# Start addresses in SBUF of the operands of the weight products, in a hybrid attention, SSD and short-convolution kernel

## The chip, the cores and the metric

The kernel runs on one core of one Trainium2 chip. The metric is the time of one execution in device microseconds. Before the change it is 1823.35 us, the median of three runs (1823.07 to 1825.55). All inputs and the output are float32.

## The reference, cut to what matters

Two layers over 256 latent tokens of width 2048, with 256 context tokens beside the first:

```
h  = modulate(rms_norm(x, g0), shift, scale)          # shift, scale, gate = split(silu(c) @ ada_w + ada_b)
hc = modulate(rms_norm(ctx, g0), shift_c, scale_c)
p  = h @ w_in ;  pc = hc @ w_in[:, COL_K:]            # w_in: 2048 x 14400
ya = neighbourhood_attention(q, k, v, k_ctx, v_ctx) * silu(gate_a)     # 16 heads of 128
yb = gated_group_rmsnorm(bidirectional_ssd(...) + d * xs, z)           # 32 heads of 64, state 128
x  = x + gate * (concat(ya, yb) @ w_out)              # w_out: 4096 x 2048
h1 = modulate(rms_norm(x, g1), shift1, scale1)
bg, cg, hv, g = split(h1 @ sc_in, 4)                  # sc_in: 2048 x 8192
x  = x + gate1 * ((silu(g) * bg * dw_conv(cg * hv)) @ sc_out)          # sc_out: 2048 x 2048
```

Nearly all of the arithmetic is in the products with `w_in`, `w_out`, `sc_in` and `sc_out`.

## The kernel before

**Products in two parts.** A float32 product is made of three products of TensorE's faster float32r type. A weight tile (1024 columns in 128 partitions, 512 KB) is loaded into a `raw` buffer, rounded to float32r by ScalarE (`split`, L399, into one of three tiles `wH`), and the rest is found by VectorE (`low_part`, L406, into one of three tiles `wL`). Activations are split in the same way into `hH[kb]` and `hL[kb]`, for the 16 blocks `kb` of 128 input channels ("k-blocks"). Then high x high, high x low and low x high are summed in a PSUM bank:

```
mm(o, actH[:, tt], H, first, False)          # mm_act: activations stationary, 512 weight columns move
mm(o, actH[:, tt], Lo, False, False)
mm(o, actL[:, tt], H, False, last)
mm(o, H[:, bb], actH[:, :n], f, False)       # mm_ws: weights stationary, n = 256 or 512 tokens move
mm(o, H[:, bb], actL[:, :n], False, False)
mm(o, Lo[:, bb], actH[:, :n], False, last)
```

`mm` is the helper at L188 that records every product, and `turn` at L192 records every transpose. `proj` walks the 16 k-blocks in order and runs one of three forms: "act" (`mm_act`: Q, K and V of the attention, the output projection, `sc_out`), a width (`mm_ws`: 512 for B, C and X of the SSD, 256 for the gates), or "both" (`mm_both`: `sc_in`, where one product of 512 columns takes the high and the low half of an `h1` tile together against `wH`, and one of 256 takes the high half against `wL`). In "act" with four token tiles a k-block holds 4 x 3 products; in the 512 and 256 forms it holds 4 column blocks x 3.

**What sets the order.** The order on every engine is written out by a planner when the program is built: `Plan` keeps a clock for each engine and marks by tile and 128-element unit; side work (norms, attention heads, SSD chunks, the gemv of `ada_w` on VectorE) stands in generators that `pump` lets in between the products when their inputs are due. `issue` sends weight loads on SP's queue as soon as a `raw` buffer is free. ScalarE's queue issues a few DMAs; GpSimd issues none. The planner sees names of tiles and offsets inside them, never an address.

**Where tiles lie.** `st(shape, tag, ...)` asks the pool `sb` for a tile with one buffer. The pool gives a tag its place when the tag is first asked for, one after another in each of the 128 partitions, and later tiles with the same tag share the place. At the bottom lie 16384 bytes that the builder keeps for descriptors of DMAs that software would generate, and four small constants. So places follow from the order of the `st` calls: first `tmp`, `half`, `raw`, `wH`, `wL` and the attention buffers; then constants; `x_load` takes `hH0` to `hH7` for the rows of x; a small tile `bs1` and `Bl`, `Cl` follow, then `hL2` to `hL15` (as `xm`, the transposed x); later, when the context rows are loaded, `hH8` to `hH15`; and at last `hL0` and `hL1`. The tags are used again and again: `xs`, `hH`, `mix0` to `mix15` and `y2` share the places of `hH`; `xm`, `hL`, `mix16` to `mix31` and `h1` those of `hL`.

## Time and profile before

| | |
|---|---|
| median of the runs | 1823.35 us (1823.07 to 1825.55) |
| span of the profiled execution | 1819.0 us; the runs' median is 4.35 us above it, for what lies around the first and the last instruction |
| instructions | 26337 |
| loads of weights into `raw`, 512 KB each | w_in 209, ada_w 163, sc_in 128, w_out 64, sc_out 32 |
| moved by DMA | 376.90 MB, 207 GB/s over the span |
| splitting a weight tile | ScalarE 1044 ns, VectorE 1213 ns (440 of each) |

How to read it: a row of the profile's groups gives line, engine, operation, output<-inputs by the program's names without their numbers, shape, count, busy time, mean time of one in ns, and the idle time of the engine just ahead of them. PE is TensorE's products; PEld is its loading of stationary operands, which runs beside them. Products are pipelined, so that one "takes" 390 ns while the next starts 227 ns after it; the pace is read from starts, or from the busy time of a stretch without gaps, divided by the products that start in it. Stretches are given in us from the span's start.

### The profile page before, as it was taken

What the parts mean: (1) busy time and instruction counts of PE and PEld (TensorE: products, weight loads), DVE (VectorE), ACT (ScalarE), POOL (GpSimd) and SP (SyncE); (2) the same over time, 40 slices, a digit from 0 to 9 for tenths busy, and PEclk for the clock granted to TensorE, in tenths of its full rate; (3) what the DMA queues carried; (4) which work ended last, traced back from release to release, by engine and by line L of the source; (5) the groups of instructions that cost most, each with busy time, mean ns of one, the idle gap of its engine ahead of it and who ended that gap; (6) DMA issues with size and microseconds to landing.
All of it is one profiled execution on the core that took longest, in us unless ns stands there. A gap on an engine that the chain in (4) does not pass through costs nothing.

```text
span 1819.0 us, 26337 instructions
## 1 busy us (share of the span) xinstructions
PE 1779.8 (98%) x9961; PEld 1484.2 (82%) x9961; DVE 1259.4 (69%) x2041; ACT 775.3 (43%) x1362; POOL 30.5 (2%) x28
## 2 busy tenths in 40 slices
PE   5999999999999999999999999999999999999998
PEld 3677888878888878888877898787878888888887
DVE  5566775887575887575887687766768866565665
ACT  5322543455232455232454344543435444444442
POOL 0000100000000000000001000000000000000000
PEclk9999999999999999999999999999999999999999
DMA  9987654566655576755575566768876776666564
GB/s 321 344 290 251 202 167 130 165 211 206 206 164 172 163 222 198 218 163 173 166 221 181 166 183 179 219 217 287 272 248 199 237 232 189 189 193 188 193 209 152
DMA packets 249216, 376.90 MB, mean 207 GB/s; under 512 B 32656, under 2 KB 104048, under 8 KB 249088
## 3 DMA queue, kind: packets, MB, share of 16 engines
q1 hardware_dynamic: 239792, 366.64, 64.2%
q10 hardware_dynamic: 9296, 8.57, 1.4%
q8 instruction: 78, 1.28, 0.3%
q14 instruction: 50, 0.41, 0.1%
HBM read 368.70 MB, written 7.77 MB: 207 GB/s over the span
## 4 chain that ended last, share of the span: by engine, by line
PE 90%; DMA 5%; DVE 3%; issue 1%; ACT 1%; SPq 0%; ACTq 0%; POOLq 0%; POOL 0%; DVEq 0%
PE bank L188 87%; DMA raw<-in_ada_w 4%; PE bank L192 3%; DVE wL L406 1%; DMA tmp<-dram_mixd 1%; DVE acc L793 1%; DMA raw<-in_w_out 1%; ACT wH L399 0%; SPq L556 0%; DVE hL L742 0%; DVE tmp L738 0%; ACT mix L1486 0%; ACT hH L736 0%; DVE xm L602 0%; DVE tmp L1780 0%
## 5 line engine op out<-in xcount | busy, mean ns | idle before, releaser
L399 ACT CAST wH<-raw 128x1024 fp32r<-128x1024 f32 (+1 forms) x440 | 459.0, 1044 | 704.3 <-PE bank L188 550.8
L406 DVE TENSOR_TENSOR wL<-raw,wH 128x1024 fp32r<-128x1024 f32 (+1 forms) x440 | 531.9, 1213 | 264.1 <-ACT wH L399 261.7
L188 PE MATMUL bank<-h,wH 128*128 128x512 f32 x1024 | 358.0, 396 | 2.7 <-ACT h L1626 1.5
L188 PE MATMUL bank<-hH,wH 128*128 128x256 f32 (+1 forms) x1040 | 353.4, 340 | 0.9 <-ACT wH L399 0.9
L188 PE MATMUL bank<-hL,wH 128*128 128x256 f32 (+1 forms) x1040 | 338.1, 325 | 0.0
L188 PE MATMUL bank<-hH,wL 128*128 128x256 f32 (+1 forms) x1024 | 330.9, 323 | 0.8 <-DVE wL L406 0.8
L188 PE MATMUL bank<-h,wL 128*128 128x256 f32 x1024 | 285.0, 278 | 0.0
L188 PE MATMUL bank<-wH,hH 128*128 128x512 f32 x640 | 258.4, 404 | 4.7 <-ACT hH L736 2.6
L188 PE MATMUL bank<-wL,hH 128*128 128x512 f32 x640 | 250.8, 392 | 0.3 <-DVE wL L406 0.3
L188 PE MATMUL bank<-wH,hL 128*128 128x512 f32 x640 | 249.8, 391 | 0.1
L793 DVE SCALAR_TENSOR_TENSOR acc<-raw,csil,acc 128x512 f32<-128x512 f32 x256 | 191.9, 749 | 64.2 <-DMA raw<-in_ada_w 50.6
L188 PEld LDWEIGHTS bank<-h,wH 128*128 128x128 f32 x1024 | 192.1, 188 | 49.4 <-issue 2.2
L188 PEld LDWEIGHTS bank<-hH,wH 128*128 128x128 f32 x1040 | 196.5, 189 | 24.5 <-issue 7.5
L188 PEld LDWEIGHTS bank<-hL,wH 128*128 128x128 f32 x1040 | 196.9, 189 | 20.2 <-issue 5.3
L188 PEld LDWEIGHTS bank<-hH,wL 128*128 128x128 f32 x1024 | 194.0, 189 | 18.2 <-DVE wL L406 1.4
L188 PEld LDWEIGHTS bank<-h,wL 128*128 128x128 f32 x1024 | 192.7, 188 | 0.0
L188 PE MATMUL bank<-wH,mix 128*128 128x512 f32 x512 | 163.1, 394 | 1.0 <-ACT wH L399 1.0
L188 PEld LDWEIGHTS bank<-wH,hH 128*128 128x128 f32 x640 | 120.2, 188 | 36.3 <-issue 7.5
L188 PEld LDWEIGHTS bank<-wH,hL 128*128 128x128 f32 x640 | 120.2, 188 | 26.2 <-DVE hL L742 0.6
L188 PEld LDWEIGHTS bank<-wL,hH 128*128 128x128 f32 x640 | 120.2, 188 | 24.7 <-DVE wL L406 1.1
L188 PEld LDWEIGHTS bank<-wH,mix 128*128 128x128 f32 x512 | 96.2, 188 | 22.1 <-ACT wH L399 1.4
L188 PE MATMUL bank<-wL,mix 128*128 128x512 f32 x256 | 100.5, 392 | 5.2 <-DVE wL L406 5.2
(244 smaller groups left out, 1661.4 us busy)
## 6 DMA issues: line engine op xcount, KB each, us to landing
raw<-in_w_in SPq DMA_DIRECT2D x209, 512.0 KB, 4.5
raw<-in_ada_w SPq DMA_DIRECT2D x163, 512.0 KB, 4.8
raw<-in_sc_in SPq DMA_DIRECT2D x128, 512.0 KB, 3.7
raw<-in_w_out SPq DMA_DIRECT2D x64, 512.0 KB, 4.3
raw<-in_sc_out SPq DMA_DIRECT2D x32, 512.0 KB, 4.5
tmp<-dram_csr SPq DMA_DIRECT2D x32, 256.0 KB, 7.3
PT<-in_ada_w SPq DMA_DIRECT2D x14, 512.0 KB, 8.4
yi<-in_ada_w SPq DMA_DIRECT2D x8, 512.0 KB
```

Source lines behind the costliest of these rows:

```text
L188: E(T.matmul(o, l, r, start=start, stop=stop, skip_group_check=True))
L192: E(T.transpose(o, i, ident if k == 128 else ident[:k, :k]))
L399: E(S.copy(H, v))
L406: E(V.tensor_tensor(out=Lo, in0=v, in1=H.bitcast(F32), op=ALU.subtract))
L793: E(V.scalar_tensor_tensor(out=acc, in0=v[:, j], scalar=csil[:, 2 * k + j:2 * k + j + 1], in1=acc, op0=ALU.mult, op1=ALU.add))
```

## The change

Right after `st` is defined, all tiles that weight products read are asked for first, so that the pool lays them out from the bottom, and a pad ahead of them brings the first to byte 2048. The scratch for software DMAs shrinks from 16384 to 1024 bytes, which makes the start of the pool 1152 and gives the room for the pad.

```
+    sb.tile([128, 224], F32, tag="pad", name="pad", bufs=1)
+    for k in range(16):
+        st([128, 512], f"hH{k}", F32R)
+    for k in range(16):
+        st([128, 512], f"hL{k}", F32R)
+    for k in range(3):
+        st([128, 1024], f"wH{k}", F32R)
+    for k in range(3):
+        st([128, 1024], f"wL{k}", F32R)
...
-    nc = bacc.Bacc("TRN2", target_bir_lowering=False, num_devices=1)
+    nc = bacc.Bacc("TRN2", target_bir_lowering=False, num_devices=1, dynamic_dma_scratch_size=1024)
```

The start addresses in a partition (bytes), as the two programs have them:

| tiles | before | modulo 2048 | after | modulo 2048 |
|---|---|---|---|---|
| `hH0` to `hH7` | 145984 and on | 576 | 2048 and on | 0 |
| `hH8` to `hH15` | 204416 and on | 1664 | 18432 and on | 0 |
| `hL0`, `hL1` | 220800, 222848 | 1664 | 34816, 36864 | 0 |
| `hL2` to `hL15` | 166528 and on | 640 | 38912 and on | 0 |
| `wH0` to `wL2` | 66688 and on | 1152 | 67584 and on | 0 |
| `tmp`, and `half` in steps of 1024 | 16512 and on | 128 | 92160 and on | 0 |
| `raw`, `KT`, `QT`, `Vt`, `PT`, `xtm`, `yi`, `sz`, `gt` | 46208 and on | 1152 | 121856 and on | 1024 |
| `Bl`, `Cl` | 162432, 164480 | 640 | 197120, 199168 | 512 |

576 is 64 more than a multiple of 128; all other rows of before are 128 more than a multiple of 512 (the odd `half` tiles, 1152, too). A weight tile's slices start 2048 bytes apart (two blocks of 512 columns), its column blocks 512 bytes apart.

No instruction is added, removed or moved: with tile numbers and line numbers left out, the rows of all five engines and of their DMA queues, with their waits, are the same in both programs.

## The prediction

> **What bounds the kernel now.** The page is read first: the span, the busy shares, the granted clock, the queues and the chain of work that ended last.

> ```profile
> span 1819.0 us, 26337 instructions
> ...
> PE 1779.8 (98%) x9961; PEld 1484.2 (82%) x9961; DVE 1259.4 (69%) x2041; ACT 775.3 (43%) x1362; POOL 30.5 (2%) x28
> ...
> PEclk9999999999999999999999999999999999999999
> ...
> q1 hardware_dynamic: 239792, 366.64, 64.2%
> q10 hardware_dynamic: 9296, 8.57, 1.4%
> q8 instruction: 78, 1.28, 0.3%
> q14 instruction: 50, 0.41, 0.1%
> ...
> PE 90%; DMA 5%; DVE 3%; issue 1%; ACT 1%; SPq 0%; ACTq 0%; POOLq 0%; POOL 0%; DVEq 0%
> PE bank L188 87%; DMA raw<-in_ada_w 4%; PE bank L192 3%; DVE wL L406 1%; DMA tmp<-dram_mixd 1%; DVE acc L793 1%; DMA raw<-in_w_out 1%; ACT wH L399 0%; SPq L556 0%; DVE hL L742 0%; DVE tmp L738 0%; ACT mix L1486 0%; ACT hH L736 0%; DVE xm L602 0%; DVE tmp L1780 0%
> ```

> TensorE is busy 98% of a span of 1819.0 us, 90% of the chain is PE, and 87% is the one helper line (L188) that records every product. The clock is granted in full in all 40 slices. So the kernel is a long row of products standing end to end, and what changes the time between the start of one product and the start of the next changes the span. VectorE (69%) and ScalarE (43%), which split the weights, run behind it. DMA holds 5% of the chain, 4% in loads of ada_w.

> Second view: the groups of products, kept apart by shape. The names are output<-stationary and moving operand in alphabetical order; a mean of one (396 ns) is a latency, since products overlap.

> ```profile
> L188 PE MATMUL bank<-h,wH 128*128 128x512 f32 x1024 | 358.0, 396 | 2.7 <-ACT h L1626 1.5 <-DVE h L1607 1.2
> L188 PE MATMUL bank<-h,wL 128*128 128x256 f32 x1024 | 285.0, 278 | 0.0
> L188 PE MATMUL bank<-wH,hH 128*128 128x512 f32 x640 | 258.4, 404 | 4.7 <-ACT hH L736 2.6 <-DVE sz L768 1.4 <-DVE gt L768 0.7
> L188 PE MATMUL bank<-wL,hH 128*128 128x512 f32 x640 | 250.8, 392 | 0.3 <-DVE wL L406 0.3
> L188 PE MATMUL bank<-wH,hL 128*128 128x512 f32 x640 | 249.8, 391 | 0.1
> L188 PE MATMUL bank<-hH,wH 128*128 128x256 f32 x640 | 184.8, 289 | 0.0
> L188 PE MATMUL bank<-hL,wH 128*128 128x256 f32 x640 | 180.7, 282 | 0.0
> L188 PE MATMUL bank<-hH,wL 128*128 128x256 f32 x640 | 180.5, 282 | 0.5 <-DVE wL L406 0.5
> L188 PE MATMUL bank<-hH,wH 128*128 128x512 f32 x400 | 168.6, 421 | 0.9 <-ACT wH L399 0.9
> L188 PE MATMUL bank<-wH,mix 128*128 128x512 f32 x512 | 163.1, 394 | 1.0 <-ACT wH L399 1.0
> L188 PE MATMUL bank<-hL,wH 128*128 128x512 f32 x400 | 157.4, 394 | 0.0
> L188 PE MATMUL bank<-hH,wL 128*128 128x512 f32 x384 | 150.5, 392 | 0.3 <-DVE wL L406 0.3
> L188 PE MATMUL bank<-wL,mix 128*128 128x512 f32 x256 | 100.5, 392 | 5.2 <-DVE wL L406 5.2
> L188 PE MATMUL bank<-wH,y 128*128 128x512 f32 x256 | 79.2, 390 | 0.0
> L188 PE MATMUL bank<-wL,y 128*128 128x512 f32 x128 | 50.0, 391 | 0.0
> L192 PE MATMUL bank<-const,tmp 128*128 128x128 f32 x324 | 45.6, 272 | 0.2 <-ACT KT L952 0.2
> ...
> L188 PE MATMUL bank<-PT,Vt 128*128 128x256 f32 x128 | 29.8, 380 | 0.0
> ```

> The products of split weights are 5280 of 512 columns (1024 with h; 3 x 640 with activations stationary; 400 + 400 + 384 with weights stationary; 512 + 256 with mix; 256 + 128 with y) and 2944 of 256 columns (1024 with h, 3 x 640). All have a new stationary operand. PE's idle time ahead of them is a few us in all, so nothing is left to gain there by waiting less.

> Third view: busy time in chosen stretches. Each stretch was cut, by the starts in the timeline, to hold whole k-blocks of one stream; the number of products that start in it follows from the loops, and the count in brackets also holds those still running at an edge.

> ```profile
> core 0: us, PE busy (x), PEclk, DMA share, GB/s
> 0.00:80.00 80.00, 58.24 (x434) 1.00 1.00 329
> 1018.58:1032.64 14.06, 14.06 (x61) 1.00 0.60 187
> 1038.11:1054.43 16.32, 16.32 (x74) 1.00 0.68 199
> 1055.84:1062.91 7.07, 7.07 (x63) 1.00 0.44 143
> 1065.82:1070.12 4.30, 4.30 (x39) 1.00 0.66 181
> 1725.96:1736.96 11.00, 11.00 (x50) 1.00 0.49 172
> 1736.96:1747.85 10.89, 10.89 (x49) 1.00 0.59 200
> 1424.69:1469.92 45.23, 45.23 (x258) 1.00 0.74 244
> 1493.01:1725.96 232.95, 232.95 (x1346) 1.00 0.61 190
> ```

> Read in pairs, first half of the k-blocks against the second. (1) Weights stationary, 512 columns: k-blocks 3 to 7 take 14.06 us for 60 products, 234.3 ns each; k-blocks 10 to 15 take 16.32 us for 72, 226.7 ns each. (2) The same with 256 columns: k-blocks 1 to 5, 7.07 us for 60, 117.8 ns; 8 to 10, 4.30 us for 36, 119.4 ns. (3) Activations stationary, sc_out: k-blocks 0 to 7, 11.00 us for 48, 229.2 ns; 8 to 15, 10.89 us for 48, 226.9 ns. (4) The sc_in stream, pairs of a 512- and a 256-column product: early, 45.23 us for 128 pairs, 353.4 ns a pair; from 1493.01 us on, 232.95 us for 1343 products, 346.9 ns a pair, with tiles at unchanged places. In (1) to (3) the code of both halves is the same line; what differs is the tile. By the table of start addresses, hH0 to hH7 (and what reuses them: mix0 to 7, y2_0 to 7) lie 64 bytes off a multiple of 128, and hH8 to hH15, all hL and all wH and wL on one. So the trace of before already holds both classes.

> **The change, part by part.** *Instructions.* None is added, removed or moved on any engine: the order depends on names of tiles and offsets in them, not on addresses. No wait changes. What moves is where tiles lie.

> *Scratch of 1 KB.* The queues listed are hardware ones and the instruction fetch; none is fed by software from POOL. [...]

> *hH0 to hH7 leave the 64-byte class.* I take the second half's rows for them.
> - Weights stationary, 512 columns: half of 400 + 400 + 384, 592 products, x (234.3 - 226.7) = 4.5 us less.
> - Activations stationary: half of 3 x 640, 8 of the 32 mix tiles in 768, half of 256 + 128, so 960 + 192 + 192 = 1344, x (229.2 - 226.9) = 3.1 us less.
> - Weights stationary, 256 columns: half of 3 x 640 = 960, x (119.4 - 117.8) = 1.5 us more. This class loses.

> Together 6.1 us less. In the first 80 us PE is busy 58.24 with the DMA share at 1.00, so there the products wait for loads; some 240 of the 1344 run there or soon after, 0.5 us, which I take off: **5.6 us** is left.

> *All other operands go from 128 to 0 past a multiple of 512.* No row shows a product operand there. The nearest rows are those of the second half, which stay at what they are: 0. The bounds come from the spread between classes: as good as the best rows in every stream (the fast cycle in sc_in throughout: at most 352 pairs run before 1493 us, x 6.5 ns, 2.3 us less), or as bad as the worst (below, 11.4 us more). One reason keeps me near 0: distances between operands. In the second half w and hH and hL already agree modulo 512, as everything will after, and a w slice 640 past 2048 meets an hL at 640 (the very same place) within the 226.7 ns stretch.

> *Everything else that shifts* (raw, tmp, banks of bias, const). VectorE and ScalarE work beside PE; a few per cent on them stay hidden while DVE is at 69%. A few per cent on the loads that hold 5% of the chain would be 91 us x 3% = 3 us, either way; I take 0.

> [...]

> *Sum.* The profiled execution: 1819.0 - 5.6 = 1813.4 us of span. The runs' median, 1823.35, is 4.35 above the span, for what lies around it; so **1817.8 us**.

> **The rivals.**

> *N, addresses are not the cause.* The halves would differ through what runs beside them, and the time stays 1823.35. For it: pair (4) shows 6.5 ns a pair of difference with unmoved tiles, so the row of products can settle into different rhythms by itself. Against it: in sc_out the slow half has the lower DMA share (0.49 against 0.59), and the 1.6 ns of pair (2) goes the other way, which a busier neighbour would not do.

> *B, the 128 bytes past 512 cost every product something, and 0 does not.* Rows that could show the size:

> ```profile
> 280.05 1.89 PE L188 MATMUL bank<-PT,Vt 128*128 128x256 f32 x8
> ...
> 1001.96 0.60 PE L192 MATMUL bank<-const,tmp 128*128 128x128 f32 x4
> ```

> [...] I spread B between 12 and 88 us less. [...]

> *S, slower: a start at 0 is itself a bad class, as 64 is.* Then the second half falls to the first half's rows: 592 x 7.7 = 4.5, and 960 + 576 + 192 = 1728 products x 2.3 = 4.0; 960 x 1.6 = 1.5 comes back; and sc_in runs in its slow cycle for the other 671 pairs, x 6.5 = 4.4. Together 11.4 us more, 1834.8. For it: of the two classes of place that the trace shows, one is bad for no reason that it shows. It decides where k-blocks 8 to 15 of the 512-column stream rise above 230 ns.

> *The change does not do what it says.* Its addresses can be read off the program, and are as stated; I give this nothing.

> **How the numbers follow.** The forecast (first half like the second) 0.50; its own range is 1815 to 1823, the gain being eaten if sc_in takes its slow cycle throughout (4.4 us). N 0.18, B 0.15, S 0.17. A measurement of this kernel tells 0.2%, 3.6 us, from no change. Three quarters of the forecast lie beyond that: faster 0.375 + 0.15, about 0.53; same 0.125 + 0.18, about 0.30; slower 0.17. Range 1790 to 1831: it takes the forecast and N whole, B down to 33 us (about 0.11 left below), and S up to two thirds (0.07 left above).

> **What would show it.** In the same stretches of the changed kernel: forecast, k-blocks 3 to 7 of the 512-column stream at 227 ns, sc_out's first half at 10.89 us, 256 columns at 119.4 in both halves. N: the first half still at 234 and 11.00. B: 220 or less in both halves. S: 230 or more in the second. What would make the prediction wrong without any of these is a new rhythm: sc_in at neither 353.4 nor 346.9 ns a pair, since its 1024 pairs move the span by 1 us for each ns.

## The result, and the profile after

| | runs | median, us | lowest to highest |
|---|---|---|---|
| before, beside it | 6 | 1823.21 | 1819.66 to 1825.55 |
| after | 6 | 1816.65 | 1813.18 to 1819.18 |

The ratio is 0.9966, 95% interval 0.9952 to 0.998: faster by 0.34%. The forecast was 1817.8 us. The profiled execution of the changed kernel took 1814.06 us, its span 1812.3 (before: 1819.0).

The page of the changed kernel, the same rows as before (all line numbers are 10 higher, so the product helper is L198):

```profile
span 1812.3 us, 26337 instructions
...
PE 1775.1 (98%) x9961; PEld 1487.4 (82%) x9961; DVE 1259.2 (69%) x2041; ACT 775.3 (43%) x1362; POOL 30.5 (2%) x28
...
PE 92%; DMA 3%; DVE 2%; issue 1%; ACT 1%; SPq 0%; POOL 0%; POOLq 0%; DVEq 0%; ACTq 0%
```

Of the 6.7 us by which the span is shorter, 4.7 are PE's busy time (1779.8 to 1775.1) and 2.0 its idle time (39.2 to 37.2). No other engine's busy time moved by more than 0.2 us, apart from PEld, which runs beside PE. In the chain, DMA's share went from 5% to 3%.

The stretches of the prediction again, in the changed kernel, holding the same products. Columns: length, PE's busy time and the products seen in it, granted clock, share of the DMA engines, GB/s.

```profile
core 0: us, PE busy (x), PEclk, DMA share, GB/s
0.00:80.00 80.00, 59.94 (x442) 1.00 0.96 337
1013.05:1026.65 13.60, 13.60 (x62) 1.00 0.60 186
1032.09:1048.41 16.32, 16.32 (x74) 1.00 0.60 197
1049.84:1057.04 7.20, 7.20 (x62) 1.00 0.48 146
1059.92:1064.24 4.32, 4.32 (x38) 1.00 0.65 181
1719.62:1730.53 10.91, 10.91 (x51) 1.00 0.51 172
1730.53:1741.41 10.88, 10.88 (x50) 1.00 0.60 201
1418.35:1463.58 45.23, 45.23 (x258) 1.00 0.75 244
1486.66:1719.62 232.96, 232.96 (x1346) 1.00 0.61 190
```

In order: with weights stationary and 512 columns, k-blocks 3 to 7 fell from 14.06 to 13.60 us (60 products, 226.7 ns each), and 10 to 15 stayed at 16.32. With 256 columns, k-blocks 1 to 5 rose from 7.07 to 7.20 (120.0 ns), 8 to 10 from 4.30 to 4.32. In sc_out the first half fell from 11.00 to 10.91, the second from 10.89 to 10.88. sc_in shows both its rhythms, and in these two stretches they are unmoved: 45.23 us for 128 pairs, 232.96 for 1344 products.

Over all products: the time from each start to the next, by stream, averaged without the intervals that contain a stall (over 250 ns at 512 columns, 140 at 256; for sc_in, both kinds of product together), and the difference times the number of products.

| stream | products | before, ns | after, ns | change, us |
|---|---|---|---|---|
| weights stationary, 512 columns | 1184 | 230.8 | 227.9 | -3.5 |
| activations stationary (w_in) | 1920 | 228.9 | 227.8 | -2.1 |
| activations stationary (mix) | 768 | 227.7 | 227.2 | -0.4 |
| activations stationary (sc_out) | 384 | 227.8 | 226.7 | -0.4 |
| weights stationary, 256 columns | 1920 | 118.8 | 119.8 | +1.9 |
| sc_in | 2048 | 174.4 | 174.0 | -0.7 |
| sum | | | | -5.2 (by unrounded means) |

So about 5.2 us are the pace of these products, and 1.5 of the 6.7 lie elsewhere, mostly in waits.

### The profile page after: what moved, and what is told of

Read it like the earlier page. It is cut to its first block, busy times and chain, and to the rows that moved or that the text cites. A ratio compares the mean times of both kernels' runs of the same rounds, so it can differ in the third digit from the quotient of the medians.

```text
span 1812.3 us, 26337 instructions
## 1 busy us (share of the span) xinstructions
PE 1775.1 (98%) x9961; PEld 1487.4 (82%) x9961; DVE 1259.2 (69%) x2041; ACT 775.3 (43%) x1362; POOL 30.5 (2%) x28
## 3 DMA queue, kind: packets, MB, share of 16 engines
q1 hardware_dynamic: 239792, 366.64, 63.8%
q10 hardware_dynamic: 9296, 8.57, 1.4%
q8 instruction: 78, 1.28, 0.3%
## 4 chain that ended last, share of the span: by engine, by line
PE 92%; DMA 3%; DVE 2%; issue 1%; ACT 1%; SPq 0%; POOL 0%; POOLq 0%; DVEq 0%; ACTq 0%
PE bank L198 90%; PE bank L202 3%; DMA raw<-in_ada_w 2%; DVE wL L416 1%; DVE acc L803 1%; DMA tmp<-dram_mixd 0%; DMA tmp<-dram_csr 0%; DVE hL L752 0%; SPq L566 0%; ACT wH L409 0%; DVE tmp L748 0%; ACT hH L746 0%; DVE xm L612 0%; ACT mix L1496 0%; DVE tmp L1790 0%
## 5 line engine op out<-in xcount | busy, mean ns | idle before, releaser
L198 PE MATMUL bank<-h,wH 128*128 128x512 f32 x1024 | 357.2, 395 | 2.7 <-ACT h L1636 1.5
L198 PE MATMUL bank<-hH,wH 128*128 128x256 f32 (+1 forms) x1040 | 352.6, 339 | 0.9 <-ACT wH L409 0.9
L198 PE MATMUL bank<-hL,wH 128*128 128x256 f32 (+1 forms) x1040 | 336.9, 324 | 0.0
L198 PE MATMUL bank<-hH,wL 128*128 128x256 f32 (+1 forms) x1024 | 331.2, 323 | 0.5 <-DVE wL L416 0.5
L198 PE MATMUL bank<-h,wL 128*128 128x256 f32 x1024 | 284.5, 278 | 0.0
L198 PE MATMUL bank<-wH,hH 128*128 128x512 f32 x640 | 257.4, 403 | 4.8 <-ACT hH L746 2.6
L198 PE MATMUL bank<-wL,hH 128*128 128x512 f32 x640 | 249.8, 391 | 0.3 <-DVE wL L416 0.3
L198 PE MATMUL bank<-wH,hL 128*128 128x512 f32 x640 | 249.3, 390 | 0.1
L198 PEld LDWEIGHTS bank<-h,wH 128*128 128x128 f32 x1024 | 192.1, 188 | 49.1 <-issue 2.2
L198 PEld LDWEIGHTS bank<-hH,wH 128*128 128x128 f32 x1040 | 197.8, 190 | 23.2 <-issue 7.5
L198 PEld LDWEIGHTS bank<-hL,wH 128*128 128x128 f32 x1040 | 197.9, 190 | 19.8 <-issue 5.3
L198 PEld LDWEIGHTS bank<-hH,wL 128*128 128x128 f32 x1024 | 194.6, 190 | 16.5 <-DVE wL L416 1.1
L198 PEld LDWEIGHTS bank<-h,wL 128*128 128x128 f32 x1024 | 192.4, 188 | 0.0
L198 PE MATMUL bank<-wH,mix 128*128 128x512 f32 x512 | 164.1, 397 | 2.2 <-ACT wH L409 2.2
L198 PEld LDWEIGHTS bank<-wH,hH 128*128 128x128 f32 x640 | 120.2, 188 | 35.6 <-issue 7.5
L198 PEld LDWEIGHTS bank<-wH,hL 128*128 128x128 f32 x640 | 120.1, 188 | 25.4 <-DVE hL L752 0.6
L198 PEld LDWEIGHTS bank<-wL,hH 128*128 128x128 f32 x640 | 120.2, 188 | 24.3 <-DVE wL L416 1.1
L198 PEld LDWEIGHTS bank<-wH,mix 128*128 128x128 f32 x512 | 96.9, 189 | 23.4 <-ACT wH L409 2.7
L198 PE MATMUL bank<-wL,mix 128*128 128x512 f32 x256 | 100.6, 393 | 3.8 <-DVE wL L416 3.8
```

Of the source, the lines that this page charges most:

```text
L198: E(T.matmul(o, l, r, start=start, stop=stop, skip_group_check=True))
```

## The experiments

All kernels below have the instructions of before in the same order on PE; only addresses differ. "Before" is run beside each of them.

### Without any multiple of 2048, and the scratch alone

`e1_swap64`, against the kernel before: a tile of 64 bytes is asked for ahead of `hH0` to `hH7` instead of behind them, so these eight move from 576 to 640 modulo 2048, and nothing moves but them and the small tile itself.

```
+    bs1 = st([128, 16], "bs1")
     x_load(0)
...
-    bs1 = st([128, 16], "bs1")
```

> The kernel before, with the 64-byte tile bs1 asked for ahead of hH0 and not behind hH7: hH0 to hH7 go from 576 to 640 past a multiple of 2048, nothing else moves. Theory P (a product operand that starts 64 bytes off a multiple of 128 is what costs): the whole gain without any 2048-byte start, about 1817; first half of the 512-column stream 227 ns a product (234 before), of sc_out 10.89 us (11.00), of the 256-column stream 119.4 ns (117.8). Theory R (operands of neighbouring products have to agree modulo 128, whatever the value): the same here. Theory L (the multiple of 2048 counts): no gain, 1823, first half at 234.

`e2_scratch`, against the kernel before:

```
-    nc = bacc.Bacc("TRN2", target_bir_lowering=False, num_devices=1)
+    nc = bacc.Bacc("TRN2", target_bir_lowering=False, num_devices=1, dynamic_dma_scratch_size=1024)
```

> The kernel before with the scratch of 1 KB alone: every tile moves down by 15360 bytes, which changes places modulo 2048 (by 1024) and none modulo 1024. P, R: no change, 1820 to 1826, the first half still at 234 ns and 11.00 us. L: no gain either, as nothing starts at a multiple of 2048. A theory that the gain lies in the scratch itself: 1817.

Measured: `e1_swap64` 1815.96 us median of 8 runs, ratio 0.9973 (0.9958 to 0.9987). Its stretches (512 columns, k-blocks 3 to 7; 256 columns, 1 to 5; sc_out, first and second half):

```profile
core 0: us, PE busy (x), PEclk, DMA share, GB/s
1014.89:1028.49 13.60, 13.60 (x62) 1.00 0.64 192
...
1051.68:1058.88 7.20, 7.20 (x63) 1.00 0.51 148
...
1720.52:1731.43 10.91, 10.91 (x50) 1.00 0.51 167
1731.43:1742.31 10.88, 10.88 (x49) 1.00 0.63 204
```

They are those of the changed kernel to 0.01 us, and the sum over all products is -5.0 us against -5.2. **Sixty-four bytes of shift in eight tiles give the products all that the change gives them**; no tile need begin at a multiple of 2048.

`e2_scratch`: 1824.57 us median of 10 runs, ratio 1.001 (0.9998 to 1.0021). The scratch alone brings no gain. (Its profiled execution took 6260 us, so no pace is read for this kernel.)

### Place or distance

In `e1_swap64` and in the changed kernel two things are true at once: no product operand starts 64 off a multiple of 128, and all agree with one another. Two kernels separate these. `e3_all64`, against the changed kernel, moves everything behind the pad by 64 bytes, so that every product operand lies in the class of place that was slow before, and all still agree (the `raw` buffers and the other tiles behind them move by 64 as well):

```
-    sb.tile([128, 224], F32, tag="pad", name="pad", bufs=1)
+    sb.tile([128, 240], F32, tag="pad", name="pad", bufs=1)
```

> The changed kernel with a pad of 240 and not 224 elements: every operand of the weight products starts 64 past a multiple of 2048, all alike. P: every 512-column product is in the bad class, weights stationary 234 ns in both halves, sc_out 11.00 us in both, 1184 x 7.6 + 3456 x 2.3 = 17 us more, 1920 x 1.6 = 3 us less: about 1831. R: they agree, so all rates are those of the changed kernel: 1817. L: off 2048, so at least as slow as before.

`e4_h07_64`, against the changed kernel, moves `hH0` to `hH7` alone by 64:

```
-    sb.tile([128, 224], F32, tag="pad", name="pad", bufs=1)
-    for k in range(16):
+    sb.tile([128, 240], F32, tag="pad", name="pad", bufs=1)
+    for k in range(8):
+        st([128, 512], f"hH{k}", F32R)
+    sb.tile([128, 496], F32, tag="pad2", name="pad2", bufs=1)
+    for k in range(8, 16):
```

> The changed kernel with hH0 to hH7 alone put 64 bytes further, everything else at a multiple of 2048. P and R: the gain is gone, about 1822, first half of the 512-column stream 234 ns, sc_out 11.00 us. L: a part of the gain stays, since all other operands start at multiples of 2048: 1819 or less.

Measured: `e3_all64` 1820.21 us median of 10, ratio 0.9988 (0.9975 to 1.0001); `e4_h07_64` 1824.63 us median of 10, ratio 1.0012 (1.0003 to 1.0021). The stretches of `e3_all64`: 512 columns, k-blocks 3 to 7 and 10 to 15, then sc_out's halves.

```profile
core 0: us, PE busy (x), PEclk, DMA share, GB/s
...
1015.60:1029.20 13.60, 13.60 (x61) 1.00 0.64 191
1034.64:1050.96 16.32, 16.32 (x73) 1.00 0.62 197
...
1723.30:1734.21 10.91, 10.91 (x51) 1.00 0.56 166
1734.21:1745.09 10.88, 10.88 (x50) 1.00 0.66 206
```

And of `e4_h07_64`, the same:

```profile
core 0: us, PE busy (x), PEclk, DMA share, GB/s
1018.18:1032.18 14.00, 14.00 (x61) 1.00 0.62 187
1037.66:1053.98 16.32, 16.32 (x73) 1.00 0.64 188
...
1726.15:1737.34 11.19, 11.19 (x50) 1.00 0.54 174
1737.34:1748.25 10.91, 10.91 (x49) 1.00 0.61 194
```

With everything 64 bytes off, both halves run at 226.7 ns: **place as such costs the products nothing**. With half of the tiles off against the others, the first half is back at 233.3 ns and sc_out at 233.1, worse than its 229.2 before. Before, `hH0` lay 64 bytes *below* a multiple of 256 from the weights, in `e4_h07_64` it lies 64 *above* one, so in sc_out the sign matters as well.

`e3_all64` also shows that the median holds more than the pace: its products gain 5.2 us, as the changed kernel's do, its span only 3.0 (1816.0), and its ratio is not clear of 1. What the rest is comes further below.

### Against what the distance counts

`e5_ladder`, against the changed kernel, gives the 16 k-blocks of `hH` and of `hL` sixteen different starts, the weights staying at 0:

```
+    steps = [0, 32, 64, 96, 128, 160, 192, 224, 256, 320, 384, 512, 576, 1024, 1088, 1536]
...
+            shift(f"{c}{k}", steps[k] - (steps[k - 1] if k else 0))
             st([128, 512], f"h{c}{k}", F32R)
```

> The changed kernel with the tiles of k-block 0 to 15 (hH and hL alike, so h1, mix and y2 too) put 0, 32, 64, 96, 128, 160, 192, 224, 256, 320, 384, 512, 576, 1024, 1088, 1536 bytes past a multiple of 2048, and wH and wL at a multiple: a scale for the distance between activations and weights, read by k-block in one run. The earlier runs left theory R, distance and not place, since a kernel with all operands at 64 had the rates of the changed kernel. R with 128 as the period: 512-column stream 227 ns a product at 0, 128, 256, 384, 512, 1024, 1536; near 234 at 64, 192, 320, 576, 1088; something between at 32, 96, 160, 224. R with a longer period (512 or 2048): 128, 256 and 384 are bad as well. A period under 64, or place modulo 128 alone: the 64s differ from that.

`e6_w64`, against the changed kernel, puts 64 bytes ahead of the weight tiles: every `wH` and `wL` lies 64 past every activation (and all that follows them moves by 64, the `raw` buffers too).

```
+    sb.tile([128, 16], F32, tag="pad2", name="pad2", bufs=1)
     for k in range(3):
         st([128, 1024], f"wH{k}", F32R)
```

> The changed kernel with wH and wL alone put 64 bytes further; all activations stay at a multiple of 2048, so moving operands agree with moving ones and stationary with stationary ones, and each product's two operands are 64 apart. Theory M (moving against stationary operand): both halves in the bad class, sc_out 11.00 us in both halves, 512-column stream 230 to 234 ns, 256 columns 117 to 118 ns; 3456 x 2.3 + 1184 x 3 to 7 less 1920 x 2 ns, about 8 to 12 us over the changed kernel, 1825 to 1829. Theory N2 (neighbouring moving operands, hH against hL): the rates of the changed kernel, 10.89 us in all of sc_out and 227 ns, 1817.

Measured: `e5_ladder` 1829.87 us, ratio 1.0038 (1.0024 to 1.0052). Nearly every k-block averages between 228 and 234 ns, those at 0, 256, 1024 and 1536 too; only the one at 512 comes near 227, in sc_out (227.2). So it did not settle the period: with 12 products to a k-block and another distance in the next, each change seems to cost some products until the pace settles (the k-block at 256 ran at 226.7 ns only in its last nine). As a ladder it was badly built.

`e6_w64` 1825.23 us median of 10, ratio 1.0017 (1.0002 to 1.0033). Its stretches: 512 columns, k-blocks 3 to 7 and 10 to 15; 256 columns, 1 to 5 and 8 to 10; sc_out, second half; sc_in, early and late.

```profile
core 0: us, PE busy (x), PEclk, DMA share, GB/s
1017.58:1031.58 14.00, 14.00 (x61) 1.00 0.61 187
1037.18:1053.98 16.80, 16.80 (x73) 1.00 0.66 198
1055.40:1062.46 7.06, 7.06 (x62) 1.00 0.43 139
1065.29:1069.37 4.08, 4.08 (x38) 1.00 0.68 181
...
1739.76:1750.74 10.98, 10.98 (x49) 1.00 0.60 197
1422.95:1468.17 45.22, 45.22 (x258) 1.00 0.77 244
1491.33:1728.77 237.44, 237.44 (x1347) 1.00 0.62 186
```

All activations agree with one another here, and all weights do; still every stream has moved. So what counts is the distance between moving and stationary operands. (Whether it is a product's own stationary operand or the next one's, which is loaded beside it, PEld being busy 1487.4 of 1812.3 us in the changed kernel, was not tried: the stationary operands of a stream all lie alike here.) And it has more than one price: 233.3 ns in all k-blocks with the weights stationary, but 228.8 in sc_out, where the weights move (10.98 us for 48); **256 columns are faster than at distance 0**, 117.7 ns and then 113.3 (4.08 us for 36); and sc_in stays in its slow rhythm to the end, 237.44 us for 1344 products, 353.3 ns a pair.

### The distances, one projection at a time

`e7_by_proj` keeps one distance through a whole projection. The weight tiles become 1152 values long, and a split writes at an offset that belongs to the projection, so that its weights start that many bytes later than a multiple of 256, where all activations start.

```
+    def distance(w, c0):
...
+        if w is sc_out:
+            return 64 + 64 * (c0 // 512)
+        return 0
...
-        H = WH[k % NW][:, :nb * n].rearrange("p (b c) -> p b c", b=nb)
+        z = apart[k] // 4
+        H = WH[k % NW][:, z:z + nb * n].rearrange("p (b c) -> p b c", b=nb)
```

> The changed kernel with weight tiles of 1152 columns, in which each projection's weights start a chosen number of bytes further (the rest of the layout agrees modulo 512): gates 0, 64, 128, 192 and z 32, 96, 160, 224 (256-column stream); C 32, 96, 160, 224 and X 64, 128, 192, 256 (512 columns, weights stationary); Q, K, V of groups 1 to 3 32, 64, 96, 128, 160, 192, 224, 256, 0; sc_in 0 to 224 in steps of 32, twice; sc_out 64, 128, 192, 256. A clean scale: one distance holds through a whole projection. Theory R128 (period of 128 bytes): 0, 128, 256 give 226.7 ns at 512 columns, 64 and 192 the rates of the run with the weights at 64 (ws 233, act 229). Theory R256: 128 is as bad as any, 256 gives 226.7 (the k-block at 256 in the first scale had 226.7 in its last nine products). 256 columns: 114.8 at 64 and 119.8 at 0 under both, at 192 119.8 or more under R256 and 114.8 under R128.

Measured: 1823.48 us (one run; before 1823.17). Its stretches: first three 512-column projections with the weights stationary and 128, 192 and 256 bytes later (k-blocks 10 to 15, 72 products), then sc_out's four projections at 64, 128, 192 and 256, with the weights moving (48 products each).

```profile
core 0: us, PE busy (x), PEclk, DMA share, GB/s
570.12:586.84 16.72, 16.72 (x73) 1.00 0.51 157
844.77:861.26 16.49, 16.49 (x74) 1.00 0.53 161
1037.16:1053.49 16.33, 16.33 (x73) 1.00 0.61 196
1738.62:1749.60 10.98, 10.98 (x49) 1.00 0.64 208
1760.75:1771.90 11.15, 11.15 (x49) 1.00 0.80 246
1783.10:1794.30 11.20, 11.20 (x49) 1.00 0.79 248
1794.30:1805.19 10.89, 10.89 (x49) 1.00 0.51 177
```

Written as (moving start - stationary start) modulo 256, both forms lie on one line. Where the weights are stationary and start 192 later, the moving operand is 192 below, which is 64 modulo 256.

| moving - stationary, modulo 256 | weights stationary, ns | weights moving, ns |
|---|---|---|
| 0 | 226.8 | 226.9 |
| 64 | 229.0 | 228.8 |
| 128 | 232.2 | 232.3 |
| 192 | 233.3 (`e6_w64`) | 233.3 |

The theory of a period of 128 (R128) falls, since 128 is among the worst; that of 256 (R256) holds, 256 being as good as 0. With it the k-blocks of `e5_ladder` that lie 64 past a multiple of 256 read well afterwards: 229.3 to 230.5 ns with the weights stationary (in X), 232.8 to 233.5 with the weights moving in sc_out. One reading is off the line: in `e4_h07_64`, weights stationary, the products with `hH` are at 64 and that with `hL` between them at 0, and they take 233.3, not 229.0. Before, the same three stood at 192, 0, 192 and took 234.3. A distance that changes from product to product seems to cost by itself, as in the ladder; that was not tried alone. The streams of 256 columns follow another scale: over whole projections 119.8 ns at 0, 114.7 with the weights 64 later, between 116.8 and 119.9 at the other multiples of 32. There R256 missed as well: for 192 it had said 119.8 or more, and it is 116.8.

The table is no slope. Q, K and V of the groups 1 to 3 had their weights (moving) at odd multiples of 32 too. Two stretches without a stall, with the weights 96 and 160 later (143 and 46 products):

```profile
core 0: us, PE busy (x), PEclk, DMA share, GB/s
...
461.47:494.84 33.37, 33.37 (x144) 1.00 0.68 210
652.81:663.59 10.78, 10.78 (x48) 1.00 0.72 230
```

That is 233.4 and 234.3 ns; over whole projections, without stalls, 32 gives 233.4 and 224 gives 232.9. So at 512 columns every odd multiple of 32 is slower than 64, and of the distances tried only 0 and 256 run at 227 ns.

### A distance for each projection

If 512 columns are best at 0 and 256 columns with the weights 64 later, each projection can have its own. `e8_gates64` is built as `e7_by_proj`, with

```
+    def distance(w, c0):
+        return 64 if w is w_in and COL_G <= c0 < COL_K else 0
```

> The same with the weights of gates and z alone 64 bytes further, everything else at distance 0: the 256-column stream at 114.8 ns in place of 119.8, 1920 products, 9.6 us less than the changed kernel; all other streams as there. About 1807, ratio to the kernel before 0.991. If the rate of a stream depended on places and not on the distance within the stream, it would stay at 119.8 and 1817.

`e9_after` is the changed kernel once more, run beside it:

> The changed kernel once more beside these, for the comparison on one chip: 0.9966 of the kernel before, 1815 to 1817.

Measured: `e8_gates64` 1812.44 us median of 6, ratio to before 0.9941 (0.9919 to 0.9964); `e9_after` 1813.93, 0.995 (0.9931 to 0.9969). The 256-column mean fell from 119.8 to 116.9 ns, 5.5 us over 1920 products. The expectation had the count wrong: C, too, enters in products of 256 columns, as the gates and z do (the section on the kernel puts it with the 512-column ones by mistake), so only 1536 of the 1920 were moved. The intervals of the two kernels overlap, so the times alone don't tell `e8_gates64` from the changed kernel. The rest of what is missing is a second rhythm, seen in the 256-column k-blocks 1 to 5 and 8 to 10:

```profile
core 0: us, PE busy (x), PEclk, DMA share, GB/s
...
1046.22:1053.28 7.06, 7.06 (x62) 1.00 0.50 151
1056.25:1060.33 4.08, 4.08 (x38) 1.00 0.68 186
```

117.7 ns in the first, 113.3 in the second, at one distance, as in `e6_w64`. `e10_gzc64` moves C as well, with weight tiles of 1536 values, so that all of them start alike modulo 2048:

```
-        return 64 if w is w_in and COL_G <= c0 < COL_K else 0
+        return 64 if w is w_in and (COL_G <= c0 < COL_K or COL_C <= c0 < COL_DT) else 0
```

> The changed kernel, with the split weights that follow the gates, z and C (all that enter products of 256 columns with the weights stationary, 1920 of them) 64 bytes on from where a multiple of 256 would put them, the others and all activations at multiples of 256; the weight tiles are 1536 values long, so that all of them begin alike modulo 2048. Theory R256 (the period depends on moving start minus stationary start modulo 256): 1920 x (119.8 - 114.8) = 9.6 us below the changed kernel of the same call, 1814.5 - 9.6 = about 1804.9 us, ratio to before 0.990, the other products as in the changed kernel (227 to 228 ns at 512 columns). If the first six k-blocks of each projection stay in the slower rhythm (117.8) whatever the tiles' starts: 116 ns on average, 7.3 us, 0.9915. If the gain of the 64 bytes was only that of the gates and z of the run before (C at 119.8): 1536 x 5 = 7.7 us, 0.991. If placing does nothing beyond the changed kernel: 0.995.

`e11_scin224` takes sc_in out of its slow rhythm besides:

```
+        if w is sc_in:
+            return 224
```

> As the run beside it, with the weights of sc_in 224 bytes on as well. There the pairs of a 512-column and a 256-column product take 353.4 ns in the first 80 us of that projection in the changed kernel and 346.9 ns after them; at 224 bytes apart the run by projections showed 346.7 ns. Theory R256: the slow rhythm is gone, about 226 pairs x 6.5 ns = 1.5 us less than the run beside it and 346.7 ns in all pairs, ratio to it 0.999. Rival: the rhythm of the pairs is chosen by how the stream begins and not by the distance, so that any part of the projection may fall in either: between 0 and 3.4 us more than the run beside it (512 pairs x 6.5 ns).

Measured: `e10_gzc64` 1810.77 us median of 6, ratio 0.9926 (0.9905 to 0.9947); `e11_scin224` 1808.3 us median of 6, ratio 0.9925 (0.9903 to 0.9948). In `e10_gzc64`, 256 columns, k-blocks 8 to 10, and the stretch of its profiled execution in which the granted clock fell:

```profile
core 0: us, PE busy (x), PEclk, DMA share, GB/s
...
1055.88:1060.12 4.24, 4.24 (x39) 1.00 0.69 185
...
1100.00:1200.00 100.00, 94.61 (x440) 0.97 0.64 189
```

And in `e11_scin224`: the same k-blocks, then sc_in early (128 pairs) and late.

```profile
core 0: us, PE busy (x), PEclk, DMA share, GB/s
...
1055.62:1059.70 4.08, 4.08 (x38) 1.00 0.67 176
1411.70:1456.07 44.37, 44.37 (x258) 1.00 0.77 251
1478.81:1711.77 232.96, 232.96 (x1347) 1.00 0.63 190
```

The 256-column mean is 116.2 ns in both, some 7 us below the changed kernel's over 1920 products. That is the expectation's second case (the first k-blocks stay in the slower rhythm), not its first. The tiles' starts modulo 2048 don't choose the rhythm: k-blocks 8 to 10 take 4.24 us in the one run and 4.08 in the other, at the same addresses. sc_in early went from 45.23 to 44.37 us, 346.6 ns a pair; over the whole stream the run saved 1.4 us, where 1.5 was expected. Summed by stream, the products of `e11_scin224` take 13.5 us less than before, against 5.2 for the change. The medians say 5.6 us between it and `e9_after`, which was run in another series, and the intervals of their ratios overlap a little: a gain over the changed kernel is shown by the pace, and by the times it is not beyond doubt. In the profiled execution of `e10_gzc64` the granted clock hides part of the gain: eleven products between 1125 and 1161 us took 427 ns each instead of 227, 2.2 us.

### What is left: the waits

From before to after 1.5 us of 6.7 are not in the pace. By how many us the start of the same product is ahead of the kernel before, in the profiled executions:

| product | before, at us | after | `e9_after` | `e1_swap64` | `e3_all64` |
|---|---|---|---|---|---|
| 250th | 51.8 | 1.7 | 2.9 | 0.0 | 0.4 |
| 6000th | 1064.2 | 6.0 | 6.1 | 4.1 | 3.1 |
| 7000th | 1250.9 | 4.2 | 7.2 | 3.9 | 1.0 |
| last | 1813.2 | 6.8 | 8.8 | 5.9 | 3.1 |

Between the 250th and the 6000th the four gain 4.3, 3.2, 4.1 and 2.7 us; most of the rest comes from two places where PE waits, the first 52 us (in the changed kernel 14.2 us for loads of ada_w) and the stretch around the output projection (1064 to 1251 us). There two executions of one and the same program, after and `e9_after`, differ by 1.2 and by 3 us. The medians of `e1_swap64` (1815.96) and `e3_all64` (1820.21), which were run side by side, still differ by 4 us with the same pace of products, though the intervals of their ratios overlap.

A part of this is the granted clock. In the output projection, before and after, each stretch right behind PE's waits there:

```profile
core 0: us, PE busy (x), PEclk, DMA share, GB/s
1162.00:1172.00 10.00, 8.25 (x40) 1.00 0.64 199
1159.70:1163.10 3.40, 3.40 (x9) 0.50 0.76 211
```

In the changed kernel seven products from 1159.8 us on took 427 ns each instead of 227, 1.4 us in all, at half the clock. `e9_after` and `e3_all64` have such a stretch there too, with six and seven products; before and `e1_swap64` have none. Whether the change has to do with it is not shown.

Whether the loads' targets, which lie 64 bytes off in `e3_all64` alone of these four, cost something was not tried by itself. In `e6_w64` they lie so as well, and there the span grew by 3.2 us, the sum of the products by 2.3. It stays open.

## Why the prediction was right

**What bounds the kernel.** Right. The profile's page gives 4.7 us of the 6.7 to PE's busy time, and no other engine changed.

**The forecast, half by half.** "First half like the second" came true in every stretch that was named: 226.7 ns for 234.3, 10.91 us for sc_out (10.89 was forecast), 120.0 in both halves at 256 columns (119.4 was forecast).

**The terms.** Weights stationary at 512: 4.5 us forecast, 3.5 measured. This term was too large, because its 234.3 ns came from five k-blocks in a settled stretch, while over all first halves, with side work cut in, it was nearer 233.9 before and 228.2 after, and not 226.7. Activations stationary: 3.1 forecast, 2.1 + 0.4 + 0.4 = 2.9 measured. 256 columns: 1.5 more forecast, 1.9 measured. sc_in: 0 forecast, within a bound of 2.3 less, and 0.7 less measured: the stretch from 1373 to 1405 us was already in the fast rhythm after the change. The rest: 0, within 3 us either way, and 1.5 less measured, with 3.8 less in `e9_after` and 2.2 more in `e3_all64`. The pace, 5.6 us forecast (6.1, less 0.5 for products that wait for loads) and 5.2 measured, and the rest, 0 forecast and 1.5 measured, made up for each other: that the time came within 1.2 us of the forecast is luck, since `e9_after`, the same kernel, gained 3.8 us outside the pace.

**The reason.** Half right, and this is what the experiments changed. The prediction put the cost on the place of a tile, 64 bytes off a multiple of 128. `e3_all64` has every operand at such a place at no cost. It is the distance between a product's two operands, modulo 256, and it was in the trace of before: the sentence on operands that agree, given as a reason to expect nothing from moving 128 to 0, named what the experiments show to be the cause. Before, `hH0` to `hH7` at 576 stood against weights at 1152, that is 192 with the weights stationary and 64 with the weights moving. The table of `e7_by_proj` prices these at 233.3 and 228.8; the prediction's rows were 234.3 and 229.2.

**The rivals.** N (not the addresses) falls by `e1_swap64`, whose only edit is 64 bytes: its first half runs at 226.7 ns, where before had 234.3. B (128 past 512 costs every product something) falls: the second half stayed at 226.7. No run shows a cost of 128 past 512, so B's spread of 12 to 88 us, and the 33 us and the 0.11 that the range takes from it, were the author's estimate alone; what the runs showed in its place is 16.32 us for k-blocks 10 to 15 both at 128 and at 0. S (0 is itself bad) falls in the same row. What could have made the prediction wrong without these, sc_in in another rhythm, did not happen by this change, but it can: in `e6_w64` that stream stays slow to the end, at 353.3 ns a pair.

**Readings that were off.** None of them changes the forecast. In the rows of the products the moving operand comes first and the stationary one second: `bank<-wH,hH` with 512 columns has the activations stationary. C is a stream of 256 columns, not of 512, and B and C hold two column blocks to a k-block. The row of `PT` and `Vt` (1.89 us for eight, less the 380 ns of the last) gives 215.7 ns for a plain fp32 product of 256 columns, where one of split weights takes 119.4; it does not tell what a place costs. The late sc_in pairs take 346.7 ns, not 346.9, since the stretch began a quarter of a microsecond ahead of its first product. And S cut at two thirds leaves 0.06 above the range, not 0.07.

## What to carry to other kernels

Where a row of products stands end to end, compare the pace of the same line over different tiles; a few per cent between them can be addresses (here 234.3 against 226.7 ns). What counts here is the moving slice's start minus the stationary slice's, modulo 256 bytes (226.9 ns at 0, 228.8 to 233.3 at 64, 128 and 192), so a stray 64-byte tile between two groups is enough (`e1_swap64` moved one, and the first half went to 226.7 ns); give both groups the same remainder, and try other remainders for the narrow products by themselves (256 columns: 119.8 ns at 0, 116.2 with the weights 64 later). Vary one distance for a whole stream, not from block to block, and judge by the pace in the trace: with gains of 5 us, the medians of two kernels with the same pace still differed by 4.
